# A decoder block on one core: the load of the first block of attention's output moves ahead of w_out's stored parts in the queue

## The chip, the cores and the metric

The kernel runs on one core of one Trainium2 chip. A core has five engines that each work through their own list of instructions in order: PE (matrix multiplications; PEld is its loading of weights), DVE (vector), ACT (scalar and activation), POOL, and SP, which here only issues transfers between the chip's large memory and the on-chip memory. An engine waits on semaphores that other engines and transfers raise; an instruction that waits holds up all that stands behind it on its engine. The metric is the device time of the program in microseconds (us), median of several runs. The clock of PE can be throttled, and the profile gives the granted clock as a share of full speed.

## The reference: one decoder block

The block has 1024 tokens of width 1024, in float32. Its first half is a mixture of two kinds of attention, its second an MLP of width 4096:

```python
h = rms_norm(x, g_attn_pre) * (1 + sc_a) + sh_a
proj = h @ w_in                                   # q, k, v of both mixers; rotary on q and k
oa = banded_attention(qa, ka, va, 127, sink=sink_a)      # mixer A: 8 heads, window 128
ob = dilated_mixture_attention(qb, kb, vb)               # mixer B: 8 heads, three strides
mixed = concatenate([rms_norm(oa, g_mix_a), rms_norm(ob, g_mix_b)])
y = mixed @ w_out
x = x + gt_a * rms_norm(y, g_attn_post)
h = rms_norm(x, g_mlp_pre) * (1 + sc_m) + sh_m
y = square(relu(h @ w_up)) @ w_down
x = x + gt_m * rms_norm(y, g_mlp_post)
```

The modulations sh, sc and gt come from a small product of a conditioning vector with w_ada. The statement that concerns this change is `y = mixed @ w_out`, the output projection, at the border between attention and the MLP.

## The kernel before: how the work is tiled and ordered

**Precision.** Every matrix operand is split into a rounded part and the rest (hi and lo). A product is three matrix multiplications: hi by hi, hi by lo, lo by hi. The kernel text calls the hi part `oh`, `ph`, `hw[:, k, 0]`, the lo part `ol`, `hw[:, k, 1]` and so on. ACT makes the hi part by a rounding copy, DVE the rest by a subtraction.

**Stages.** The input projection (tiles `pj`) goes through the columns of w_in; its results are normalised by rotary, split and sent in pieces, through transfers by SP, into the tiles `kt` and `qt` of the attention (line 818). Attention goes through heads and blocks: scores `s_ps` (1139), the exponential on ACT (1165, 1214), normalisation on POOL (1170), transposes `pt_ps` (1244, 1247), their split `ph` on ACT (1258) and DVE (1262), and the products with v, `o_ps` (1274 to 1279). For mixer B the two halves of `o_ps` are added (`otmp` on ACT at 1306, `ot` on DVE at 1310) and stored by SP in the memory as `o_dram` (1313). v itself comes from the projection by `vt` (840), four transposes (846) and a split (854, 857).

**The output projection.** `out_block(tb)` does block tb of 128 tokens, eight in all. SP loads the attention's output of the block from `o_dram` into the tile `o_sb` (line 1486; 512 KB); ACT rounds it to `oh` (1498), DVE makes `ol` (1504), ACT squares the tile (1506), DVE adds the squares (1510, 1511), PE sums them over the partitions into `pm_o` (1517), and DVE and POOL make the inverse root from that (1525, 1527). PE computes 16 triples of 128x512, hi by hi, hi by lo and lo by hi (1545, 1546, 1547); ACT (1560) and DVE (1566) evacuate them, scaled. Then come the norm, the gate (1600), the addition of x (1603, x loaded at 1490 as `x_sb2`), the store of the new x (1605), the norm of the MLP's input (1573, 1611), eight transposes `px` (1620) and their evacuation (1636, 1639), and with that the MLP can start on this block. The first block uses a small buffer pool of its own, `early`, so that it can run while attention is still going on. w_out lies in eight pairs of tiles: the first four k are loaded raw and split on the chip (1402), the last four were split and stored in the memory before, and are loaded as pairs, 512 KB each (`wo_dram`, 1417).

**What sets the order.** Not the text of the program: a Python scheduler (class `Sched`) is run when the kernel is built. Every step has an engine, an estimated duration, the steps it depends on, the buffers that it takes and gives, and a priority (`prio`, small is first). The scheduler keeps a clock for each engine and a model of the transfers, and gives out, again and again, the step that can start first; among those of one engine with the same start the smaller `prio` wins (`pick`, line 263). The result is a fixed list of instructions for each engine. The engines keep to it, each in order. For the transfers on SP the model is 0.62 us per issue, and the bytes one after the other at a fixed rate (`give_out`, 240). So a priority on SP changes the time at which the model sees a load landed, and with it the places of all the steps that hang on it, on every engine. The MLP's order is not touched by that apart from buffers.

The priorities of SP's loads around the change are: q and k pieces -12 (818), w_out's loads -8 (1402, 1417), the gate -7 (1395), the output's loads -6 (1493), the stores of `o_dram` -5 (1313), x -3 (1490), the stores of the new x -2 (1605).

Of the kernel before, what the change touches and what calls it, by code (L numbers as in the profile page):

```python
# [177 lines left out]
class Sched:  # L178
# [21 lines left out]
    def op(self, eng, dur, emit, deps=(), **kw):  # L200

        o = self.step(dur, emit, deps, **kw)
        o.alts = None
        if isinstance(eng, str):
            self.queue[eng].append(o)
        else:
            o.alts = dict(zip(eng, zip(dur, emit)))
            for e in eng:
                self.queue[e].append(o)
        return o.ev  # L210
# [147 lines left out]
def hybrid_block(ctx: ExitStack, tc: tile.TileContext, x, positions, w_ada, b_ada, g_attn_post, w_in, w_out,  # L358
# [100 lines left out]
    def load(emit, nbytes, deps=(), takes=(), prio=5, gives=(), after=None, n=1):  # L459
        return op("SP", nbytes / (345e3 if prio > -500 else 370e3), emit, deps, takes=takes, prio=prio, gives=gives, after=after, n=n)  # L460
# [155 lines left out]
    def f_sin():  # L616
# [5 lines left out]
                prio=1)  # L622
# [89 lines left out]
    def tables(groups, place, r_place, r_bank, bank, deps):  # L712
# [30 lines left out]
       prio=8)  # L743
# [709 lines left out]
    def feed_out():  # L1453
        tb = ph2.tb
        if not hasattr(ph2, "e_wo") or todo_dense or tb and ph2.opened.t is None:
            return False
        if tb < TB and st.att >= enough[tb // 2] and len(sc.pe.get("dense", [])) <= 17:
            out_block(tb)
            ph2.tb += 1
        return ph2.tb == TB  # L1460
# [12 lines left out]
    def out_block(tb):  # L1473
# [3 lines left out]
        r_o1, r_o2 = (ph2.r_o, ph2.r_ow) if tb else (ph2.r_early, ph2.r_early)  # L1477
# [10 lines left out]
        def f_lx():  # L1488
            b["xt"] = stage("x_sb2") if r_x2 is r_stg else early.tile([P, 1024], F32, name="x_sb2", tag="early")
            nc.sync.dma_start(b["xt"][:], x[tb * P:(tb + 1) * P])  # L1490
        deps = [e_ for k_, e_ in e_o.items()
                if (items[k_][1] if items[k_][0] > 1 else items[k_][1] // 2) == tb // 2]
        el = load(f_lo, 524288, deps, takes=[(r_o1, 1)], prio=-6)

        def f_oh():
            b["oh"] = by_k(place("oh"))
# [3 lines left out]
        if not tb:  # L1500
# [4 lines left out]
                prio=2)  # L1505
# [30 lines left out]
        for n, m, k in order:  # L1536
# [19 lines left out]
            if m == 0:  # L1556
                def f_ya(c0=c0, n=n):
                    if n == 0:
# [3 lines left out]
                           takes=[] if n else [(ph2.r_y, 1)], gives=[(r_b, 1)], prio=0)  # L1562
# [61 lines left out]
        for kg in range(2):  # L1624
# [3 lines left out]
            def f_ev(eng, kg=kg, q=q):  # L1628
                def f():
# [14 lines left out]
                   takes=[(r_h2, 2)] if tq == 0 else [], gives=[(r_t, 1)], prio=1)  # L1644
# [534 lines left out]
```

## Time and profile before

| | |
|---|---|
| time, median of 3 runs | 1128.47 us (1128.34 to 1129.39) |
| time of the profiled execution | 1129.15 us |
| span of the profiled execution, first to last instruction | 1127.1 us |
| mean granted clock of PE in it | 0.996 |
| busy: PE, DVE, ACT, POOL | 1107.0, 817.2, 636.8, 255.4 us |
| transfers | 193.69 MB, mean 172 GB/s |

The span is cut by stage: the input projection and the attention run until about 385 us, the output projection, interleaved with the last attention, from there to about 505 us, and the MLP after that. The profile's views used below are these. The page gives the busy time of each engine. A table by windows gives for each stretch the busy time of each engine with the number of instructions, the granted clock and the share of the transfer engines. A timeline lists one engine's instructions by start time, with the idle time ahead of one in brackets and what ended it (`<-`). The chain of waits follows the end back from cause to cause. Matmuls are pipelined: one is shown as 0.39 us long, while the next starts 0.23 us after it, so for PE the starts are to be read, not the lengths.

### The profile page before, as it was taken

Reading aid. Unit: us, or ns where it says so; the run is one execution under the profiler, and the core shown is the slowest. Engines: PE = TensorE matmul, PEld = TensorE weight load, DVE = VectorE, ACT = ScalarE, POOL = GpSimd, SP = SyncE. Lnnn points to the kernel's source line nnn. Section 1 sums busy time; section 2 is a strip of 40 time slices with the busy share of each in tenths; the row PEclk is TensorE's granted clock in tenths of the full one; section 3 lists DMA queues with packets and bytes.
Section 4 is the critical chain, followed back from the end, with each engine's and each line's share of the span. In section 5 each row is a group of like instructions: output and inputs, shape, how many; then the busy total and the mean of one; then the engine's idle time right before and its main releaser. Section 6 shows DMA issues by size and latency. Waiting matters only on the chain.

```text
span 1127.1 us, 15613 instructions
## 1 busy us (share of the span) xinstructions
PE 1107.0 (98%) x5417; PEld 920.9 (82%) x5417; DVE 817.2 (73%) x1379; ACT 636.8 (56%) x1111; POOL 255.4 (23%) x336
## 2 busy tenths in 40 slices
PE   8999999999999999999999999999999999999997
PEld 6788888888888788788888888888888888888885
DVE  7968767666686576579889564798743996537998
ACT  8769767455665576677575334653145632246542
POOL 2447777567751131110000000000000000000003
PEclk9999999999999999999999999999999999999999
DMA  9564665554513642565861268711578112584104
GB/s 349 177 215 132 196 225 194 178 173 153 197 43 146 232 147 80 203 235 213 321 242 38 76 233 310 249 52 42 186 252 318 38 56 95 199 307 165 38 19 150
DMA packets 93215, 193.69 MB, mean 172 GB/s; under 512 B 8656, under 2 KB 31312, under 8 KB 93136
## 3 DMA queue, kind: packets, MB, share of 16 engines
q1 hardware_dynamic: 93136, 192.69, 49.2%
q8 instruction: 43, 0.70, 0.3%
q14 instruction: 36, 0.29, 0.1%
HBM read 141.28 MB, written 32.51 MB: 154 GB/s over the span
## 4 chain that ended last, share of the span: by engine, by line
PE 77%; ACT 7%; DVE 6%; DMA 3%; issue 3%; POOL 3%; SPq 1%; POOLq 0%; DVEq 0%; ACTq 0%
PE mlp_ps L1992 17%; PE mlp_ps L1991 17%; PE mlp_ps L1993 17%; PE pj L875 3%; PE pj L878 3%; PE pj L876 3%; PE s_ps L1139 3%; PE o_ps L1274 2%; PE y_ps L1545 2%; PE y_ps L1547 2%; PE y_ps L1546 1%; PE pt_ps L1244 1%; ACT p_sb L1214 1%; PE pt_ps L1247 1%; DMA o_sb<-o_dram 1%
## 5 line engine op out<-in xcount | busy, mean ns | idle before, releaser
L1991 PE MATMUL mlp_ps<-hw 128*128 128x512 f32 x896 | 349.6, 390 | 0.0
L1993 PE MATMUL mlp_ps<-hw 128*128 128x512 f32 x896 | 348.6, 389 | 0.0
L1992 PE MATMUL mlp_ps<-hw 128*128 128x512 f32 x896 | 348.6, 389 | 0.0
L1991 PEld LDWEIGHTS mlp_ps<-hw 128*128 128x128 f32 x896 | 168.2, 188 | 35.8 <-issue 0.5
L1992 PEld LDWEIGHTS mlp_ps<-hw 128*128 128x128 f32 x896 | 168.2, 188 | 35.2 <-issue 0.5
L1993 PEld LDWEIGHTS mlp_ps<-hw 128*128 128x128 f32 x896 | 168.2, 188 | 34.9
L1755 DVE TENSOR_TENSOR hw<-w,hw 128x1024 fp32r<-128x1024 f32 x96 | 114.6, 1219 | 95.2 <-ACT hw L1748 93.2
L1748 ACT CAST hw<-w 128x1024 fp32r<-128x1024 f32 x96 | 97.6, 1048 | 130.0 <-PE mlp_ps L1993 97.5
L2101 POOL TENSOR_TENSOR st<-st,nhalf 128x1 f32<-128x1 f32 x8 | 8.0, 1011 | 592.6 <-DVE st L2099 592.6
L875 PE MATMUL pj<-hw,w_hl 128*128 128x512 f32 x240 | 101.8, 424 | 0.0
L878 PE MATMUL pj<-hw,w_hl 128*128 128x512 f32 x240 | 94.7, 394 | 0.0
L876 PE MATMUL pj<-hw,w_hl 128*128 128x512 f32 x240 | 94.3, 393 | 0.0
L1262 DVE TENSOR_TENSOR ph<-pt_ps,ph 128x512 fp32r<-128x512 f32 (+1 forms) x110 | 68.2, 647 | 24.7 <-ACT ph L1258 24.5
L1748 ACT CAST hw<-u 128x1024 fp32r<-128x1024 f32 x48 | 48.7, 1052 | 64.6 <-PE mlp_ps L1993 64.6
L1258 ACT CAST ph<-pt_ps 128x512 fp32r<-128x512 f32 (+1 forms) x110 | 57.3, 557 | 24.1 <-PE pt_ps L1247 20.3
L1755 DVE TENSOR_TENSOR hw<-u,hw 128x1024 fp32r<-128x1024 f32 x48 | 57.0, 1218 | 18.2 <-ACT hw L1748 18.2
L1165 ACT ACTIVATE p_sb<-p_sb,mn 128x128 f32<-128x128 f32 (+3 forms) x64 | 49.7, 777 | 35.1 <-DVE mn L1158 32.2
L1170 POOL TENSOR_SCALAR p_sb<-p_sb,den 128x128 f32<-128x128 f32 (+3 forms) x64 | 49.0, 771 | 74.1 <-DVE den L1168 66.3
L2049 DVE TENSOR_TENSOR yacc<-yacc,mlp_ps 128x512 f32<-128x512 f32 x96 | 62.1, 681 | 3.3 <-PE mlp_ps L1993 3.3
L1024 POOL TENSOR_TENSOR ada_acc<-ada_acc,wa_st 128x512 f32<-128x512 f32 x42 | 55.8, 1328 | 3.5
L1545 PE MATMUL y_ps<-hw,oh 128*128 128x512 f32 x128 | 52.6, 411 | 0.9 <-DVE mn L1158 0.4
L878 PEld LDWEIGHTS pj<-hw,w_hl 128*128 128x128 f32 x240 | 45.1, 188 | 10.3
(207 smaller groups left out, 1994.1 us busy)
## 6 DMA issues: line engine op xcount, KB each, us to landing
hw<-s_dram SPq DMA_DIRECT2D x84, 512.0 KB, 4.3
wa_st<-in_w_ada SPq DMA_DIRECT2D x32, 512.0 KB, 4.3
w<-in_w_up SPq DMA_DIRECT2D x32, 512.0 KB, 5.5
w<-in_w_down SPq DMA_DIRECT2D x32, 512.0 KB, 6.8
s_dram<-hw SPq DMA_DIRECT2D x28, 512.0 KB, 3.2
qt<-hl SPq DMA_DIRECT2D x40, 256.0 KB, 2.6
w_st<-in_w_in SPq DMA_DIRECT2D x36, 256.0 KB, 3.1
x_sb<-in_x SPq DMA_DIRECT2D x16, 512.0 KB, 5.6
```

The source lines that it names most:

```text
L875: T.matmul(ps, w[:, 0, n], h[0], start=(k == 0), stop=False)
L876: T.matmul(ps, w[:, 1, n], h[0], start=False, stop=False)
L878: T.matmul(ps, w[:, 0, n], h[1], start=False, stop=(k == KC - 1))
L1258: A.copy(b["ph"][:, 0, :w], b["pt"][:, :w])
L1262: V.tensor_tensor(b["ph"][:, 1, :w], b["pt"][:, :w], b["ph"][:, 0, :w].bitcast(F32), ALU.subtract)
L1545: T.matmul(ps[:], b["oh"][:, k], wh[:, c0:c0 + 512], start=(k == 4 * m), stop=False)
L1748: A.copy(out[j][0], flat(src[j]))
L1755: V.tensor_tensor(out[j][1], flat(src[j]), out[j][0].bitcast(F32), ALU.subtract)
L1991: T.matmul(ps[m][:], sh, mh, start=starts and k == 0, stop=False, **kw)
L1992: T.matmul(ps[m][:], sh, ml_, start=False, stop=False, **kw)
L1993: T.matmul(ps[m][:], sl, mh, start=False, stop=k == 3, **kw)
L2049: e = op("DVE", t_dv(512), lambda: V.tensor_tensor(y(), y(), ps[m][:], ALU.add), [e, ml.e_y[tb, n]], gives=gives, prio=1)
```

## The change

One priority: for the first block (tb = 0) the load of `o_sb` has -14 instead of -6, which is ahead of all other loads of that stage. The other seven blocks keep -6.

```diff
         deps = [e_ for k_, e_ in e_o.items()
                 if (items[k_][1] if items[k_][0] > 1 else items[k_][1] // 2) == tb // 2]
-        el = load(f_lo, 524288, deps, takes=[(r_o1, 1)], prio=-6)
+        el = load(f_lo, 524288, deps, takes=[(r_o1, 1)], prio=-6 if tb else -14)
```

The scheduler makes a new list from it on every engine, from about 373 us of the run until the MLP begins. Three places of the difference (a line with - stands only before, with + only in the change) follow. First SP, at the place where the first block's output is loaded; `wo_dram` is w_out's stored part, `hl` the split q and k, `o_dram` the attention's output:

```order
 L818 DMA kt<-hl 32x2x512
+L1486 DMA o_sb<-o_dram_110 128x8x128
+L818 DMA qt<-hl 32x2x1024 x2
+L818 DMA kt<-hl 32x2x512
 L1417 DMA hw<-wo_dram_0_177 128x1024
 L1417 DMA hw<-wo_dram_1_178 128x1024
-L818 DMA qt<-hl 32x2x1024 x2
-L818 DMA kt<-hl 32x2x512
-L1486 DMA o_sb<-o_dram_110 128x8x128
 L1313 DMA o_dram_113<-ot 64x256
```

The load of `o_sb` moved ahead of two loads of w_out, two of `qt` and one of `kt`; the two of w_out come behind these. The second place is ACT, at the end of attention:

```order
 L1258 CAST ph<-pt_ps 128x512
 L1258 CAST ph<-pt_ps 128x384
-L1306 COPY otmp<-o_ps 64x256
-L1258 CAST ph<-pt_ps 128x512
-L1258 CAST ph<-pt_ps 128x384
-L1306 COPY otmp<-o_ps 64x256
-L1258 CAST ph<-pt_ps 128x512
-L1258 CAST ph<-pt_ps 128x384
 L1498 CAST oh<-o_sb 128x1024
+L1306 COPY otmp<-o_ps 64x256
+L1258 CAST ph<-pt_ps 128x512
+L1258 CAST ph<-pt_ps 128x384
```

The rounding of `o_sb` (1498) now stands ahead of two `otmp` and two pairs of `ph`, which belong to attention; behind the shown pair the square of the tile (1506) and `vt` (840) follow, and only then the second pair. The third place is PE, at the end of the input projection:

```order
 L878 MATMUL pj<-hw,w_hl 128x512
-L1274 MATMUL o_ps<-ph,v_hl 128x256 x2
-L1279 MATMUL o_ps<-ph,v_hl 128x256 x2
+L875 MATMUL pj<-hw,w_hl 128x512
+L876 MATMUL pj<-hw,w_hl 128x512
+L878 MATMUL pj<-hw,w_hl 128x512
+L1545 MATMUL y_ps<-hw,oh 128x512
+L1546 MATMUL y_ps<-hw,oh 128x512
+L1547 MATMUL y_ps<-hw,ol 128x512
+L1274 MATMUL o_ps<-ph,v_hl 128x256 x2
+L1279 MATMUL o_ps<-ph,v_hl 128x256 x2
+L846 MATMUL pv<-head,vt 128x128 x4
```

The last triple of the input projection and the first of the output projection (1545 to 1547) moved ahead of a group of attention's products with v, and v's four transposes (846) moved behind that group's first half.

## The prediction

> **What bounds the kernel now.** First the busy times on the page:
>
> ```profile
> span 1127.1 us, 15613 instructions
> PE 1107.0 (98%) x5417; PEld 920.9 (82%) x5417; DVE 817.2 (73%) x1379; ACT 636.8 (56%) x1111; POOL 255.4 (23%) x336
> ```
>
> PE is busy for 98% of the span, so a change that removes no matrix work can win only what PE loses. 1127.1 - 1107.0 = 20 us is all the idle time there is, most of it far from this change. Second, the same by stage. The columns are the stretch, its length, the busy time of PE, PEld, DVE, ACT and POOL with counts, the granted clock of PE, the DMA share and GB/s:
>
> ```profile
> 380.00:390.00 10.00, 8.78 (x43) 6.94 (x42) 5.54 (x11) 4.88 (x8) 0.00 (x0) 0.83 0.71 247
> 410.00:414.00 4.00, 3.56 (x17) 2.53 (x15) 3.96 (x11) 3.26 (x5) 1.01 (x1) 1.00 0.39 134
> 460.00:465.00 5.00, 3.83 (x20) 2.94 (x18) 3.55 (x7) 1.53 (x3) 0.83 (x2) 1.00 0.01 2
> 520.00:540.00 20.00, 20.00 (x92) 16.48 (x93) 20.00 (x26) 14.34 (x25) 0.00 (x0) 1.00 0.70 265
> 540.00:900.00 360.00, 360.00 (x1586) 297.36 (x1585) 253.59 (x260) 178.68 (x239) 0.00 (x0) 1.00 0.51 180
> ```
>
> Between 340 and 520 these three stretches, 380 to 390, 410 to 414 and 460 to 465, hold nearly all that PE loses. From 520 to 900 PE is full, in the order that it has in both kernels, so what is won before passes to the end. (DVE is full too in 520:540; a rival uses that.) Third, the chain of waits through the first place. The columns are start, length, and what ran:
>
> ```profile
> 376.33 6.03 DMA o_sb<-o_dram
> 382.37 1.05 ACT oh L1498
> 383.45 1.24 DVE ol L1504
> 384.73 0.51 PE y_ps L1547
> ```
>
> This is the load that is changed: issued at 376.33, landed at 382.37, then rounded by ACT, its rest taken by DVE, and PE waits for both. The timeline of PE there (start, length, line, and in brackets the idle time before and what ended it):
>
> ```profile
> 379.10 0.40 PE L1274 MATMUL o_ps<-ph,v_hl 128*128 128x256 f32 x2
> 379.98 0.41 PE L1244 MATMUL pt_ps<-head,p_sb 128*128 128x128 f32 x2
> ...
> 381.47 0.28 PE L1274 MATMUL o_ps<-ph,v_hl 128*128 128x256 f32 x1
> 382.01 0.38 PE L1274 MATMUL o_ps<-ph,v_hl 128*128 128x256 f32 x1 [0.25 <-DVE ph L1262]
> ...
> 383.47 0.50 PE L1545 MATMUL y_ps<-hw,oh 128*128 128x512 f32 x1 [0.44 <-ACT oh L1498]
> ...
> 384.73 0.51 PE L1547 MATMUL y_ps<-hw,ol 128*128 128x512 f32 x1 [0.53 <-DVE ol L1504]
> 385.07 1.10 PE L846 MATMUL pv<-head,vt 128*128 128x128 f32 x4
> ```
>
> From 381.47 to 385.07 PE does one group of pv and one triple of the output projection in 3.60 us. Without waits the group takes 379.98 - 379.10 = 0.88. A triple takes 0.68, from the rows of PE at 459:
>
> ```profile
> 459.49 0.39 PE L1545 MATMUL y_ps<-hw,oh 128*128 128x512 f32 x1
> ...
> 460.17 0.39 PE L1545 MATMUL y_ps<-hw,oh 128*128 128x512 f32 x1
> ...
> 461.30 0.39 PE L1547 MATMUL y_ps<-hw,ol 128*128 128x512 f32 x1
> 462.86 0.58 PE L1517 MATMUL pm_o<-ones,o_sb 128*128 128x1 f32 x4 [1.17 <-DVE o_sb L1511]
> ```
>
> So the waits at the first block cost 3.60 - 0.88 - 0.68 = **2.04 us**, more than the idle brackets add up to. Right behind them the granted clock falls (windows of 0.5 us, columns as above):
>
> ```profile
> 385.00:385.50 0.50, 0.50 (x3) 0.44 (x3) 0.00 (x1) 0.50 (x1) 0.00 (x0) 0.59 0.14 55
> 385.50:386.00 0.50, 0.50 (x5) 0.50 (x4) 0.20 (x1) 0.27 (x1) 0.00 (x0) 0.50 0.16 47
> ...
> 388.50:389.00 0.50, 0.50 (x4) 0.38 (x3) 0.00 (x0) 0.00 (x0) 0.00 (x0) 1.00 0.94 328
> ```
>
> It stays at half until 388.5. PE is busy all through these 3.4 us and does half of the work that it could: **1.7 us** lost to the clock. Together the place costs 3.74 us. The later two: at 462.86 PE starts 1.56 us behind the start before it where 0.23 is the spacing, 1.33 lost; 410:414 shows 0.44 idle.
>
> **The change, part by part.** (a) The load starts earlier. SP's issues now (start, length, line):
>
> ```profile
> 372.57 0.57 SPq L818 DMA_DIRECT2D kt<-hl  x1
> 373.23 1.04 SPq L1417 DMA_DIRECT2D hw<-wo_dram  x2
> 374.37 1.22 SPq L818 DMA_DIRECT2D qt<-hl  x2
> 375.63 0.59 SPq L818 DMA_DIRECT2D kt<-hl  x1
> 376.33 1.18 SPq L1486 DMA_DIRECT2D o_sb<-o_dram  x1
> ```
>
> In the new order o_sb stands behind the first kt, ahead of two loads of w_out, two qt and one kt, so it is issued at 373.2 instead of 376.33: 3.1 us earlier. Its bytes move while the queue is still nearly empty. How long a load of this tile takes, over its eight blocks (min, median, max):
>
> ```profile
> DMA to landing us min/median/max: 4.0/4.7/7.6
> ```
>
> I take 4.4, since nothing is ahead of it but the qt and kt behind it share the engines: landed at 377.6. Bounds 4.0 (377.2) and 6.03, as today (379.2). What the step moves besides: q and k keep their place within 1 us, and the two parts of w_out go from 373.2 to about 376.3. The first block takes the other four parts of w_out first, eight triples; with nothing in between these last 5.4 us from 379.8 on, to 385.2, and even with the slowest landing above, 7.6, the moved parts are there at 383.9. So the cover for this move is the eight triples; without them it would cost up to 4 us.
>
> (b) ACT and DVE are in order, and the new order puts the first block's work ahead of attention's. The rows of ACT and DVE that matter:
>
> ```profile
> 377.11 0.37 ACT L1306 COPY otmp<-o_ps 64x256 f32<-64x256 f32 x1 [1.64 <-PE o_ps L1277]
> 377.57 0.97 ACT L1258 CAST ph<-pt_ps 128x512 fp32r<-128x512 f32 x2
> 382.37 1.05 ACT L1498 CAST oh<-o_sb 128x1024 fp32r<-128x1024 f32 x1 [0.77 <-DMA o_sb<-o_dram]
> 384.71 1.06 ACT L1506 ACTIVATE o_sb<-o_sb 128x1024 f32<-128x1024 f32 x1 [0.41 <-DVE ol L1504]
> 383.45 1.23 DVE L1504 TENSOR_TENSOR ol<-o_sb,oh 128x1024 fp32r<-128x1024 f32 x1 [1.04 <-ACT oh L1498]
> 381.26 1.16 DVE L1262 TENSOR_TENSOR ph<-pt_ps,ph 128x512 fp32r<-128x512 f32 x2 [0.26 <-ACT ph L1258]
> ```
>
> oh now waits for the load in front of otmp and a pair of ph that are ready at 377.11 and 377.57. With landing at 377.6: oh to 378.65, otmp to 379.05, ph to 380.05; DVE does ol to 379.9, ot (0.4) to 380.35, then the ph rest. PE finishes the last projection triple at about 379.8 and starts the first output triple with no wait (it ends at 380.5; ol is there by 379.9). The pv group behind it wants the ph rest, 0.75 us after DVE begins it (382.01 - 381.26), at 381.1 instead of 380.6: 0.5 lost. The four transposes behind that want vt, which is behind the square (1.06) and takes 0.58: at 381.8 instead of 381.4: 0.4 lost. **0.9 us** instead of 3.74, if the clock stays full. At landing 4.0 the same walk gives 0.4. At 6.03: oh late by 0.6, ol by 0.8, ph by 0.9, vt by 0.3, in all 2.6, and the half clock would be likely again: 4.3, 0.6 more than now.
>
> (c) The rest of attention and of the output projection is interleaved in another way until the MLP. Today this stretch loses 0.44 + 1.33 = 1.8 us. The 462.86 kind arises where a block's load is issued only behind the store of the block ahead:
>
> ```profile
> 450.21 0.32 SPq L1605 DMA_DIRECT2D x_dram<-y_sb  x1
> 450.62 0.39 SPq L1486 DMA_DIRECT2D o_sb<-o_dram  x1
> ```
>
> That pairing is unchanged for blocks 3 to 7, so I take the same 1.8; bounds 0 and three such waits, 4.0.
>
> Sum: 1129.15 (the profiled execution, span 1127.1 plus 2.05 around it) - 3.74 + 0.9 + 0 = 1126.31. That execution stands 0.68 above the median of the runs, 1128.47; taken from there the sum gives 1125.6. I forecast **1126.0 us**, between them, since not every run need hold the 1.7 of the clock.
>
> [...]
>
> **The rivals.** (1) The stalls go, the half clock comes all the same, a few us away. For it: the clock stayed 1.00 behind a larger bracket (row 460:465). Against: it fell right behind the densest stalls. Gain 2.04 - 0.9 = 1.1: 1127.4 by the median. A gain that DVE, full in 520:540, keeps from reaching PE ends at the same place.
>
> (2) Larger gain: the front loses 0.4 and the later waits vanish too: 3.74 - 0.4 + 1.8 = 5.1 at most; with half of the later waits gone 1124.2. For it: new interleaving has more independent triples to place. Against: the unchanged pairing at 450.
>
> (3) The ACT held by the load. If it lands as late after its issue as the slowest block, 7.6 us (380.8), the walk of (b) gives 2.6 + 1.6 = 4.2, plus 1.7 of clock: 5.9 instead of 3.74, 1130.6. It decides from a landing of about 5.5 us on, where 4.2 - 2.1 + 1.7 is what the place costs today. For it: qt and kt follow at once, and over 380:390 the DMA share is 0.71. Against: the load is ahead of them.
>
> (4) Slower by the later stretch: loads of blocks 4, 5 and 6 each come behind a store and PE waits at pm_o three times (3 x 1.33 = 4.0), with the half clock behind two of them (2 x 1.7): 4.0 + 3.4 - 1.8 - 2.8 = +2.8, 1131.3. It turns slower than before once the three waits bring one drop, and measurably so with two. For it: an earlier front leaves less other work to PE there. Against: the one such wait today brought no drop.
>
> (5) The load does not land earlier, since it waits for the stores that it reads: no change, 1128.5. Against: in SP's order the kt of 372.57 already stands behind those stores, and it is issued 3.8 us ahead of o_sb.
>
> **How the numbers follow.** Forecast 0.42, (1) 0.20, (2) 0.13, (3) 0.10, (4) 0.10, (5) 0.05. No change is what lies within 0.2%, 2.26 us (1126.2 to 1130.7), about what a measurement can tell. The forecast's own range is 1124.9 to 1127.1, with some 0.7 of it below 1126.2. Faster: 0.7 x 0.42 + 0.13 = 0.42. Slower: (4) and half of (3), 0.15. Same: the remaining 0.43. The range leaves out the ends of (2) and (4): 1123.9 to 1130.2.
>
> **What would show it.** Right: SP issues o_sb at 373 to 374, ACT's oh starts at 377 to 378.5, PE's first output triple has no bracket, the windows between 380 and 390 show clock 1.00 and PE busy above 9.4. The MLP's first matmul comes 2 to 3 us earlier and the rest keeps its length. Wrong: a landing above 5.5 us; otmp or ph late by more than 2 us with brackets on pv; a clock of 0.50 anywhere in 370 to 520; pm_o brackets that sum to more than 2 us.

## The result, and the profile after

The changed kernel takes **1124.39 us** (1124.11 to 1125.35, 6 runs) against 1128.40 us of the kernel before in the same comparison (1127.03 to 1129.39, 6 runs): a ratio of 0.9970, 95% interval 0.9959 to 0.9982. A second comparison, in the experiments below, gives 1124.50 against 1127.31, ratio 0.9975 (0.9964 to 0.9986). So it is faster, by 4.0 and 2.8 us. Forecast was 1126.0, a gain of 2.5 from the median, within 1123.9 to 1130.2.

The profiled execution took 1124.29 us, its span is 1122.4, 4.7 shorter than before. PE's waits between 340 and 520, for each kernel one answer (what waited, for what, us in total, times, longest). Before:

```profile
PE pm_o L1517 <- DVE o_sb L1511: 1.2, 1, 1.2
PE y_ps L1547 <- DVE ol L1504: 0.5, 1, 0.5
PE y_ps L1545 <- DVE mn L1158: 0.4, 1, 0.4
PE y_ps L1545 <- ACT oh L1498: 0.4, 1, 0.4
PE s_ps L1139 <- DVE mn L1158: 0.3, 1, 0.3
PE o_ps L1274 <- DVE ph L1262: 0.3, 1, 0.3
PE px L1620 <- ACT xn L1611: 0.2, 1, 0.2
```

After:

```profile
PE pm_o L1517 <- DVE o_sb L1511: 0.4, 1, 0.4
PE s_ps L1139 <- DVE mn L1158: 0.3, 1, 0.3
PE px L1620 <- ACT xn L1611: 0.2, 1, 0.2
```

The waits for oh and ol are gone, as forecast, and so are the one for ph and one of the two for a softmax maximum (mn). The one at pm_o has shrunk; the other for mn and the one at px are the same in both kernels. The windows of the changed kernel (columns as in the prediction) that answer to those quoted there:

```profile
380.00:390.00 10.00, 9.85 (x63) 8.47 (x62) 7.87 (x25) 6.19 (x13) 2.43 (x3) 1.00 0.84 270
...
410.00:414.00 4.00, 4.00 (x21) 3.27 (x20) 3.82 (x13) 2.87 (x6) 0.62 (x2) 1.00 0.53 204
...
460.00:465.00 5.00, 5.00 (x24) 4.13 (x23) 1.49 (x4) 3.33 (x5) 1.25 (x2) 1.00 0.72 215
...
520.00:540.00 20.00, 20.00 (x90) 16.34 (x89) 20.00 (x22) 13.49 (x19) 0.00 (x0) 1.00 0.90 345
540.00:900.00 360.00, 360.00 (x1586) 297.46 (x1585) 253.75 (x262) 176.85 (x236) 0.00 (x0) 1.00 0.50 175
```

Busy rose from 8.78 to 9.85 in 380:390 and the granted clock there from 0.83 to 1.00. The chain of waits through the place:

```profile
372.00 0.57 SPq L818
372.68 4.34 DMA o_sb<-o_dram
377.05 1.06 ACT oh L1498
```

The load is issued 0.68 us after that kt (line 818) and lands in 4.34 us. And PE's timeline from the end of the input projection on:

```profile
378.99 0.40 PE L878 MATMUL pj<-hw,w_hl 128*128 128x512 f32 x1
379.22 0.39 PE L1545 MATMUL y_ps<-hw,oh 128*128 128x512 f32 x1
379.45 0.40 PE L1546 MATMUL y_ps<-hw,oh 128*128 128x512 f32 x1
379.69 0.39 PE L1547 MATMUL y_ps<-hw,ol 128*128 128x512 f32 x1
379.93 0.80 PE L1274 MATMUL o_ps<-ph,v_hl 128*128 128x256 f32 x2
380.56 0.40 PE L1279 MATMUL o_ps<-ph,v_hl 128*128 128x256 f32 x2
380.98 0.66 PE L846 MATMUL pv<-head,vt 128*128 128x128 f32 x4
```

The first output triple starts at the normal spacing of 0.23. The two pairs behind it take 0.63 and 0.42 where 0.24 is normal, 0.6 us lost together, and the four transposes follow.

**Where the 4.7 us come from.** The last projection triples before the changed place begin at 377.62 before and at 377.07 after: 0.55 us of the difference arose earlier, in rows that are the same in both kernels, and are noise of the one execution (the same row of PE's list there starts up to 1.5 us apart in the thirteen profiles of this case, and latest in this one of before). The first matmul of the MLP starts at 504.86 and 500.15, 4.71 apart, its last at 1118.34 and 1113.63, 4.71 again: nothing is added or given back in the MLP. That leaves 4.16 us between 377 and 500. The first place lost 3.74 and now loses 0.6, which is 3.1. The two later waits, counted by the spacing of the starts, lost 0.61 (412.37) and 1.33 (462.86); now one of 0.57 at 458.87 and about 0.15 are left, which is 1.2. The sum of 4.3 agrees with 4.16 within the rounding of these rows.

### The profile page after: what moved, and what is told of

It reads as the page before. It is cut to its first block, busy times and chain, and to the rows that moved or that the text cites. A ratio compares the mean times of both kernels' runs of the same rounds, so it can differ in the third digit from the quotient of the medians.

```text
span 1122.4 us, 15613 instructions
## 1 busy us (share of the span) xinstructions
PE 1104.7 (98%) x5417; PEld 919.2 (82%) x5417; DVE 817.5 (73%) x1383; ACT 636.5 (57%) x1107; POOL 255.1 (23%) x336
## 4 chain that ended last, share of the span: by engine, by line
PE 79%; DVE 7%; ACT 5%; issue 3%; POOL 2%; DMA 2%; SPq 0%; POOLq 0%; DVEq 0%; ACTq 0%
PE mlp_ps L1992 17%; PE mlp_ps L1991 17%; PE mlp_ps L1993 17%; PE pj L875 3%; PE pj L878 3%; PE pj L876 3%; PE s_ps L1139 3%; PE y_ps L1545 2%; PE y_ps L1547 2%; PE y_ps L1546 2%; PE o_ps L1274 2%; PE pt_ps L1244 1%; PE pt_ps L1247 1%; ACT p_sb L1214 1%; DMA w_st<-in_w_in 1%
```

## The experiments

Before and after differ in two things: when the load lands, and the plan of all engines that the scheduler makes from it. The first two experiments take them apart; their lists on PE, ACT, DVE and POOL are row for row those of the kernel they are made from, and only the one transfer moves on SP. In the code shown from here on, ` ...` stands for lines left out, and words behind # are notes. (With a priority of -9 instead of -14 the scheduler makes the same lists as with -14 on every engine, and with -7.5 those of before; so the jump that counts is the one over w_out's parts at -8. The q and k pieces behind it were not ready for a place ahead.)

**1. The load alone.** Before, with the transfer emitted as soon as the stores it reads are issued:

```diff
         self.slack = SLACK
+        self.early = None
 ...
             self.clk[e] = start + 0.62 * o.n
+            if self.early and all(d.t is not None and d.t + lat(d.eng, e) <= self.clk[e] for d in self.early[0]):
+                f, self.early = self.early[1], None
+                f()          # emits the transfer; the plan's own step for it then emits nothing
 ...
```

> Before's plan on PE, ACT, DVE and POOL row for row; only the transfer of the first block's o_sb is issued right behind the first kt, ahead of w_out's parts, q and k. My theory (the gain needs the new order of ACT, DVE and PE too): the load lands near 377.6 but oh stands behind the ph pair of 380.64, so it starts at about 381.6 instead of 382.37 and ol at about 382.7 instead of 383.45; the place loses about 1.0 instead of 2.0 us. If the half clock comes all the same the time is 1127.4, if it does not 1125.7. Rival (the earlier landing is all that matters): 1124.4, as with the whole change.

Measured: 1126.09 us against 1127.13 of before on that chip, ratio 0.9994 (0.9985 to 1.0003), 1.0 less in the medians, but the interval takes in no change. (One of its 11 executions, 1129.21, had a mean granted clock of 0.996, of which experiment 4 tells more.) ACT's timeline shows why the earlier load buys little (line numbers are 4 to 8 higher in this kernel):

```profile
380.07 0.97 ACT L1262 CAST ph<-pt_ps 128x512 fp32r<-128x512 f32 x2
380.92 1.06 ACT L1506 CAST oh<-o_sb 128x1024 fp32r<-128x1024 f32 x1
```

The load is issued at 372.66 there as in the changed kernel, but oh starts at 380.92, right behind the ph pair that stands ahead of it in the old order, and not at 377.05. PE still waits for ol:

```profile
PE pm_o L1525 <- DVE o_sb L1519: 1.1, 1, 1.1
PE y_ps L1553 <- DVE mn L1162: 0.4, 1, 0.4
PE y_ps L1555 <- DVE ol L1512: 0.3, 1, 0.3
...
```

The two later waits stand as in before. The rival of this experiment, that the landing is all that matters, falls; the profiled execution had a clock of 1.00 behind the place, and 1126.09 lies near the 1125.7 of that case.

**2. The plan alone.** The changed kernel, with the transfer held until w_out's two parts are issued:

```diff
+            if tb:
+                f_go()
+            else:
+                sc.held = f_go       # the transfer
 ...
                     nc.sync.dma_start(hw[:, k, i].bitcast(F32), wo_dram[k - 4][i][:])
+                if sc.held:
+                    sc.held()
+                    sc.held = None
 ...
```

> The changed kernel's plan on PE, ACT, DVE and POOL row for row; only the transfer of the first block's o_sb is held until behind qt, kt and the two parts of w_out, as before. My theory: it is issued at about 376 and lands at about 382, ACT waits for it in front of otmp and ph, and PE stands for about 5 us (2.6 at a landing of 379.2, and 2.8 later here) instead of 0.6, with a half clock of 1.7 behind it: 1129 to 1131. Rival (the new interleaving wins by itself, the load is hidden anyway): under 1127.

Measured: 1130.83 us against 1127.13, ratio 1.0029 (1.0019 to 1.0040), slower, and within the 1129 to 1131 of the theory. ACT stands in front of otmp and ph as the third rival of the prediction had it, and PE behind it.

ACT, then PE:

```profile
381.93 1.04 ACT L1509 CAST oh<-o_sb 128x1024 fp32r<-128x1024 f32 x1 [7.06 <-DMA o_sb<-o_dram]
```

```profile
383.02 0.50 PE L1556 MATMUL y_ps<-hw,oh 128*128 128x512 f32 x1 [3.71 <-ACT oh L1509]
...
384.29 0.80 PE L1558 MATMUL y_ps<-hw,ol 128*128 128x512 f32 x1 [0.40 <-DVE ol L1515]
```

And the windows behind it:

```profile
384.00:386.00 2.00, 1.72 (x5) 1.29 (x6) 2.00 (x5) 1.80 (x3) 0.00 (x0) 0.50 0.10 26
386.00:388.00 2.00, 2.00 (x12) 2.00 (x11) 0.91 (x3) 0.73 (x2) 0.00 (x0) 0.50 0.79 132
388.00:390.00 2.00, 2.00 (x10) 1.81 (x9) 1.39 (x3) 0.81 (x2) 0.00 (x0) 0.50 0.95 387
```

The half clock lasts from 383.5 until 390.3 here, 6.8 us, twice as long as in before (3.4). So neither part brings the gain alone: the old plan with the early load is at most about 1.0 us faster than before, which is not clear of no change, the new plan with the late load 3.7 us slower, and both together 2.8 to 4.0 faster. Later than the front, however, the new plan keeps what it won: this kernel, too, has no wait of y_ps for mn and only 0.4 at pm_o.

**3. The price of lateness.** The changed kernel with oh made two or three times (the same result each time), which holds otmp, ph and the square back as a later landing would, by 1.05 us a copy:

```diff
-            A.copy(b["oh"], b["ot"])
+            for i in range(1 if tb else 2):      # or 3
+                A.copy(b["oh"], b["ot"])
```

> The changed kernel with the first block's oh made twice by ACT (same result), as if the load landed 1.05 us later, at 378.1. Theory: ol ends 1.05 later and PE waits 0.7 for it, the ph rest and vt follow 1.05 late: in all 1.0 us over the changed kernel, and the clock stays at 1.00 since that wait is shorter than those of the threefold oh. Rival: it falls all the same, 2.7 over the changed kernel. Second rival: there is slack, 0 to 0.3.

> The changed kernel, with the first block's oh made three times over by ACT (same result), which puts 2.1 us ahead of otmp, ph and the square as a load would that lands 2.1 us later, at about 379.2. By the walk of the prediction the place then loses 2.6 instead of 0.6: 1126.4 if the clock stays at 1.00, 1128.1 if it falls to half behind the waits. Rival (the place has slack of its own, the delay is hidden): 1124.4 to 1125.

Measured: 1125.38 with two (1124.50 for the changed kernel beside it): 0.9 for 1.05 us of delay, forecast 1.0, and the clock stayed (1.00 from 340 to 540 in the profiled execution). With three 1127.01 on another chip, and 1126.82 in a repetition on a third: about 2.4 above the changed kernel's 1124.4 to 1124.5 on the other chips, where 2.0 was forecast for a clock that stays and 3.7 for one that falls. It fell in some executions: 6 and 3 of 11 have a mean clock of 0.996, and both profiled ones show it. The rest have medians of 1126.68 and 1126.64, about 2.2 above the changed kernel. PE with two and with three copies:

```profile
379.99 0.50 PE L1548 MATMUL y_ps<-hw,ol 128*128 128x512 f32 x1 [0.52 <-DVE ol L1505]
```

```profile
379.77 0.50 PE L1546 MATMUL y_ps<-hw,oh 128*128 128x512 f32 x1 [1.23 <-ACT oh L1499]
...
381.03 0.70 PE L1548 MATMUL y_ps<-hw,ol 128*128 128x512 f32 x1 [0.53 <-DVE ol L1505]
```

With two, only ol is late; with three oh is too. The place has no slack to speak of: of a delay of 2.1 us the whole comes out even without the fall of the clock, as the prediction's point of decision (a landing of about 5.5 us instead of 4.4) assumes.

**4. The changed kernel once more.** Beside before, in the same runs as the twofold oh.

> The changed kernel beside before on the chip of the first four experiments, where before's runs have a granted clock of 0.997 to 0.999 over the span against 0.996 in the profiled execution that the prediction was made from. Theory (before has the half clock of 385 to 388.5 in some executions only, and it is no part of the gain where it is absent): gain = front 2.0 - 0.6, later waits 1.8 - 0.7, together 2.5 us, 1124.6 if before is at 1127.1. Rival (the gain is the same everywhere, the ratio 0.997 of the first comparison less its noise): 1123.7 or less.

Measured: 1124.50 against 1127.31, a gain of 2.8, where the theory gave 2.5 and the rival 3.4 or more. The 29 executions of before on this chip fall in two groups by granted clock: 8 at 0.996 with a median of 1128.58, and 21 at 0.997 to 0.999 with 1127.06. On the chip of experiments 1 and 2 none of 29 had 0.996; on a third 5 of 27, median 1128.93 against 1127.3 for the rest. The execution that the prediction was made from, 1129.15 at 0.996, was of the first group. None of the 13 executions of the changed kernel was at 0.996.

These groups need one caution. In all thirteen profiles the clock also falls to half behind the last matmul of the MLP and stays there for the last 3.1 to 6.3 us of the span (4.7 in before, 5.0 in the changed kernel), and the mean clock has this in it. With 3.4 us of half clock inside the program the mean comes to 0.996 or 0.997, so 0.998 and 0.999 leave no room for it, but 0.997 may: the first profile of the threefold oh has 0.997 and holds such a fall. So 13 is the least number among these 85 executions of before, and of the changed kernel 12 were free of it; the last, at 0.997, was its slowest (1125.35) and is open. The half clock is real, then, and costs about 1.5 to 1.6 us where it comes (1.7 was forecast). It is no part of the difference of two medians where it stays away, and most of the way from 2.8 to 4.0 in the first comparison, where before's six times reach from 1127.03 to 1129.39, is likely due to it; the clocks of those six are not all known, so this is not shown.

**5. Is PE's idle time the cause of the half clock?** Filler matmuls where PE waits, in before (five: two ahead and three more behind; the "seven" of the expectation is a miscount) and in the threefold oh (eight: five and three):

```diff
+                first = (tb, n, k) == (0, 0, 0)
+                for i in range(2 if first else 0):               # 5 with the threefold oh
+                    T.matmul(ps[:], wh[:, 0:P], wh[:, c0:c0 + 512], start=True, stop=True)
                 T.matmul(ps[:], b["oh"][:, k], wh[:, c0:c0 + 512], start=(k == 4 * m), stop=False)
-                T.matmul(ps[:], b["oh"][:, k], wl[:, c0:c0 + 512], start=False, stop=False)
+                for i in range(4 if first else 1):
+                    T.matmul(ps[:], b["oh"][:, k], wl[:, c0:c0 + 512], start=False, stop=False)
```

> Before, with seven filler matmuls in the first output triple of the first block: two that need no oh ahead of its first matmul (overwritten), three more repeats of hi by lo ahead of its third, and one where that belongs, so that PE works where it waited for oh and ol; the first block's product for k = 0 counts hi by lo four times in one half. The waits end no earlier. Theory that the half clock of 385 to 388.5 follows from PE's idle time: the granted clock stays 1.00 there and the time falls by up to 1.7, to about 1126.8. Rival (the clock falls whatever PE does): the windows still show 0.50 and the time is 1128.4 or a little more.

> Before with its waits filled, once more beside before itself. On one chip none of 29 executions of before showed 0.996, on another 8 of 29 did, with a median 1.5 us above the rest. Theory (idle time causes the drop): the filled kernel shows 0.996 in fewer executions than before does on the same chip, and its median is that of before's executions without the drop. Rival: the same share at 0.996. If before has no drop on this chip the two do not differ and nothing follows.

> The threefold oh once more, as the partner of the filled one on one chip. It had a granted clock of 0.996 or 0.997 in 10 of 11 executions where the others had 0.997 to 0.999. Expected again mostly 0.996 to 0.997, 2.5 us over the changed kernel's 1124.5: 1127.0.

> The threefold oh with eight filler matmuls where PE waits for oh (five that need no oh, overwritten) and for ol (three more repeats of hi by lo; the first block's product for k = 0 counts it four times in one half). The waits themselves end when they did. Theory (the half clock follows from PE standing idle): the clock is 0.998 to 0.999, no window behind the place shows 0.50, and the time is 1.0 to 1.7 below the unfilled one. Rival (the drop has another cause, such as the place in the program): clock and time as without the filling.

Measured: before filled 1126.97 against 1127.13, and 1127.03 against 1127.42, no difference (0.9999 and 0.9993, both intervals hold 1). On the first of these chips 1 of 11 filled executions had 0.996 against 0 of 29 of before, on the second 1 of 11 against 5 of 27: the filler in before shows no effect. The threefold oh had 0.996 in 3 of 11 executions beside 0 of 11 of the filled one, with medians of 1126.82 and 1126.78: the forecast of 1.0 to 1.7 less is a miss, since even the unfilled one was mostly spared this time. More telling are the versions of the changed kernel side by side. The share of executions at 0.996 or less grows with PE's waits at the front: 0 of 11 with the twofold oh (0.5 us), 9 of 22 with the threefold (1.2 and 0.5), 6 of 7 in experiment 2 (3.7 and 0.4). That points to idle time as the cause; the filler, which should have settled it, has too few executions to do so. On the second chip the one filled execution of before at 0.996 was the profiled one, and it shows the drop at another place:

```profile
382.00:384.00 2.00, 1.98 (x11) 1.28 (x9) 1.14 (x1) 1.68 (x3) 0.00 (x0) 1.00 0.75 297
...
386.00:388.00 2.00, 1.98 (x12) 1.43 (x11) 1.75 (x6) 0.00 (x0) 0.00 (x0) 1.00 0.55 119
...
460.00:462.00 2.00, 0.58 (x4) 0.22 (x3) 1.46 (x3) 0.48 (x1) 0.00 (x0) 1.00 0.00 0
...
464.00:466.00 2.00, 2.00 (x6) 1.54 (x6) 0.77 (x1) 0.32 (x1) 1.33 (x1) 0.50 0.19 80
```

Where the filler stands the clock is 1.00; behind the wait at pm_o, which was not filled, it is 0.50. The drop is thus not bound to the place in the program: it followed a wait of PE in every profile that has it ahead of the MLP's end (before, experiment 2, both of the threefold oh, and this one), and not every wait has it (behind the 1.17 us at pm_o in before it stayed at 1.00).

**6. Two other plans.** The priority of -14 for all eight blocks, and the changed kernel with otmp planned ahead of oh (both shown against the changed kernel):

```diff
-        el = load(f_lo, 524288, deps, takes=[(r_o1, 1)], prio=-6 if tb else -14)
+        el = load(f_lo, 524288, deps, takes=[(r_o1, 1)], prio=-14)
```

```diff
-        el = load(f_lo, 524288, deps, takes=[(r_o1, 1)], prio=-6 if tb else -14)
+        el = load(f_lo, 524288, deps, takes=[(r_o1, 1)], prio=-6 if tb else -14,
+                  after=None if tb else lambda: setattr(el, "slack", 0.6))   # its users are planned 0.6 us later
```

> The priority -14 for the loads of all eight blocks. The front is the changed kernel's row for row; the second block's load moves ahead of the gate's, the third's ahead of a store of attention's output, and the plan between 390 us and the MLP is another. Theory (the later stretch holds 0.7 us of waits in the changed kernel, and plans differ there by about a microsecond): within 1.0 us of the changed kernel on either side. Rival (earlier loads help each block as they helped the first): 0.7 us or more faster than the changed kernel.

> The changed kernel, with the landing of the first block's load planned 0.6 us later for the steps that use it: ACT does otmp, which is ready, ahead of oh instead of behind it, and PE does v's four transposes behind both halves of the group of products with v. The queue of the load stays. Theory (the 0.6 us that the place still loses come from otmp, ph and vt behind oh): 0.4 to 0.5 us faster than the changed kernel, if the later stretch keeps its 0.7. Rival (the later stretch changes by more than that): 0.3 to 1.0 slower.

Measured: 1124.58 for all blocks, no different from 1124.50; the first block's load is the one that counts. With otmp ahead of oh 1126.39, 1.9 slower than the changed kernel, where 0.4 faster was forecast and 1.0 slower was the rival's end. The front did what it should: windows of 2 us from 376 to 394 all show PE busy for 2.00. The loss is later:

```profile
PE pm_o L1517 <- DVE o_sb L1511: 1.7, 2, 1.3
PE y_ps L1545 <- DVE mn L1158: 0.6, 1, 0.6
...
```

Those are the waits of before, back again. A shift of 0.6 us in the planned time of one load turned a plan with 0.7 us of later waits into one with more than before's 1.9, while the front got better. No version measured here beats the changed kernel; one with this front and the changed kernel's later stretch would win about 0.4 us, less than the intervals here can tell, and was not built.

## Why the prediction was right, and where it was off

- **The time.** 1124.39 lies within the stated bounds, but 0.5 below the 1124.9 to 1127.1 that the prediction gave for its own forecast, and beside the 1124.2 of its rival (2). The MLP's first matmul came 4.71 us earlier where 2 to 3 were forecast. The steps below say why.
- **(a) The load.** Right to 0.1 us: issued behind the first kt, 4.34 us to landing where 4.4 was taken. (The clock time of the issue, 372.68 instead of 373 to 374, is early by the 0.55 of noise.) Nothing was late by the move of w_out's parts: PE never waits for them.
- **(b) ACT, DVE and PE at the front.** Right in mechanism, and a little pessimistic: 0.6 us lost instead of 0.9, since ph and vt were each some 0.2 to 0.3 earlier than in the walk. That the in-order engines make the landing time decisive is shown by experiments 2 and 3 (PE waits 3.71 us for oh behind the late landing; 0.9 us are lost for 1.05 us of delay).
- **The clock term, 1.7 us.** The size is about right (1.5 to 1.6 between groups of executions), but it was entered as part of a difference that every run would show. It is in some executions of before only. By going between 1126.3 and 1125.6 the prediction took off only 0.4 of it (a gain of 2.5 from the median instead of 2.84), for the right reason and with no number for how often.
- **(c) The later stretch** is the term that was mis-sized: taken as unchanged at 1.8 us (1.9 when both waits are counted by the spacing of the starts; the prediction took the first by its idle bracket), it fell to 0.7, because in the new plan the work around block 5 stands otherwise. The pairing of store and load, on which the term was rested, is indeed unchanged (447.57 and 447.99 in the changed kernel); what differs is what ACT does between oh and the square. The chain of waits before:

```profile
456.52 1.05 ACT oh L1498
457.57 1.40 ACT h L1636 x4
458.97 1.04 ACT junk L1573 x2
460.01 0.58 ACT y_sb L1560
460.59 0.95 ACT o_sb L1506
...
462.86 0.58 PE pm_o L1517 x4
```

and after:

```profile
452.60 0.76 DVE h L1639 x3
...
455.31 1.13 DVE ol L1504
...
457.63 0.64 DVE o_sb L1510
...
458.87 0.58 PE pm_o L1517 x4
```

  Before, three other pieces of work, 3.0 us, stand on ACT between oh and the square of the same tile. After, all eight evacuations h are on DVE and the square waits only for ol. The landing is not what differs: oh starts 1.32 us behind the start of PE's px (line 1620) before and 1.36 after. That this order is the cause was read from traces and not tried by itself, but it fits seven of them: where the three pieces stand between oh and the square of block 5 (before, experiment 1, and the second plan of experiment 6) PE waits 1.17, 1.10 and 1.28 us at its pm_o, and where only y_sb does (the changed kernel twice, experiment 2) 0.41 each time; with -14 for all blocks pm_o stands further back in PE's list and does not wait. That the plan and not the landing of the first block decides it is what experiments 1 and 2 show (waits of y_ps for mn and of pm_o of 0.4 and 1.1 us with the old plan, only 0.4 at pm_o with the new).
- **Rival (1)**, the clock falling all the same, did not happen in at least 12 of 13 executions. **Rival (2)**, more gained than forecast, was half right: 1.2 of the 1.9 went, and with that it forecast the time better than the forecast did. **Rival (3)** is experiment 2 in the large, with the measured price of 0.9 per 1.05 us. **Rival (4)** did not come, but experiment 6 shows its first step: a plan that is better at the front and worse behind. **Rival (5)** is refuted by the issue at 372.68.
- Without the clock term the prediction's sum is 2.0 - 0.9 = 1.1, with the measured front 2.0 - 0.6 = 1.4; the 1.2 of the later stretch makes it 2.6, against 2.8 in the second comparison. That the forecast gain of 2.5 is so near to this 2.8 is luck: a clock term that is mostly absent there stood in for a later stretch that was taken as unchanged.

## What to carry to other kernels

Where in-order lists are planned from a model of the transfers, a load and the places of its users belong together: the early load alone brought at most about 1.0 us, the plan that trusts it lost 3.7 when the load was late, and both together won 2.8 to 4.0. Count the waits behind a re-planned place too, since they can move by more than the place itself (0.7 to over 1.9 us here), and read them from a trace, because the new list shows the order of the work but not its waits. And before a term of the granted clock enters a sum, look at the clock of more than one execution.

## What the runs showed of the hardware

The half clock came and went between executions of one and the same kernel: 0 of 29, 8 of 29 and 5 of 27 at a mean clock of 0.996 on three chips. In the profile of before the trace's record of the clock has full clock from 6.21 us on, the fall at 385.09, the return at 388.50 and the fall at the end at 1122.36; in that of the changed kernel it has full clock from 4.63 us on and one fall, that at the end, at 1117.37. In four of the profiles the half clock lasted 3.4 us from its fall to its return (385.1 to 388.5 in before, 381.2 to 384.6 and 382.3 to 385.7 with the threefold oh, 463.2 to 466.6 in the filled kernel), and 6.8 us behind the longest wait, 3.71 us (383.5 to 390.3 in experiment 2). PE was not idle all through the time ahead of these five falls: in the last 3.41 us, the length of the half clock in before, it was busy for 0.45 us in experiment 2 and 1.62 and 1.65 with the threefold oh, for 2.19 in before (381.68 to 385.09) and for 1.99 in the filled kernel:

```profile
459.78:463.19 3.41, 1.99 (x11) 1.46 (x10) 2.65 (x4) 0.70 (x1) 0.00 (x0) 1.00 0.00 0
```

A stretch of that length in before with only 1.88 us of busy time, 16.45 to 19.86, had no fall behind it, so busy time as the profile counts it does not decide alone. What else does, these runs don't show.
